# A decoder trunk on one core: order of the first attention scores, the projections' lead and the conditioning jobs

## The chip, the cores and the metric

The kernel runs on one core of a Trainium2 chip. The metric is the device time of one execution in microseconds (us), the median of several runs. A core has TensorE (matmuls, transposes), VectorE, ScalarE, GpSimd, and SyncE, whose queue issues the DMAs here.

## What is computed

One sequence of 512 tokens, width 1024, passes a state-space layer, a shared K/V projection, an attention layer of three dilated branches with 16 heads of 64, and an MLP behind each of the two mixers. Every sub-layer is normalised, shifted and scaled by vectors that come from the conditioning vector `c`, and gated by a third. Cut to what matters here:

```python
def ada_chunks(c, w, b, n):                  # conditioning: c (1, 1024), w (1024, n * 1024)
    m = jax.nn.silu(c) @ w + b
    return jnp.split(m[:, None, :], n, axis=-1)

def dilated_mixer(u, w_q, k_bands, v_bands, w_o):
    q = (u @ w_q).reshape(bsz, seq, N_BRANCHES, N_HEADS, HEAD_DIM)
    for i, (win, dil) in enumerate(DILATED_BRANCHES):
        o, l = dilated_branch(q[:, :, i], k_bands[i], v_bands[i], win // dil, dil)
        ...
    weights = jax.nn.softmax(jnp.stack(lses, axis=-1), axis=-1)
    ...

# layer 1 of reference()
    k_bands, v_bands = shared_kv(h, c, kv_g, kv_ada_w, kv_ada_b, w_kv)
    shift, scale, gate = ada_chunks(c, ada_w[layer, 0], ada_b[layer, 0], 3)
    u = rms_norm(h, ln_g[layer, 0]) * (1.0 + scale) + shift
    h = h + gate * dilated_mixer(u, attn_w_q[j], k_bands, v_bands, attn_w_o[j])
    shift, scale, gate = ada_chunks(c, ada_w[layer, 1], ada_b[layer, 1], 3)
    u = rms_norm(h, ln_g[layer, 1]) * (1.0 + scale) + shift
    h = h + gate * (jnp.square(jax.nn.relu(u @ mlp_w1[layer])) @ mlp_w2[layer])
```

The softmax over the three branches together is computed as one softmax over all their keys.

## The kernel before

Every matrix product of a layer is done as three products of a high and a low part of each operand: `linear_steps` (L813) emits them in steps of three matmuls (L827 to L829) and yields after each. Weights come in blocks of 1 MB through SyncE's queue (L789), are split on ScalarE (L799) and VectorE (L801), and are kept in a pool `W` of 13 buffers, which the projected keys, queries and values share. `next_weights(2)` loads two blocks ahead.

The attention (`attention`, L1174) interleaves two streams on TensorE. One is the **feed**: the projections of V (`proj_v`, for four heads at a time), of keys and queries (`proj_kq`, for a pair of heads: six blocks of eight steps) and at the end of the output (`out_part`). Its generator yields the assumed length of each step, 0.64 or 0.327, and `fill(t)` runs steps until `t` is used up. The other stream is the **heads**: eight pairs, each in four head steps `qb`, one for each block of 128 queries. A head step makes the transposes of the softmax (`attn_turn`, L1142 and L1144, copied by L1147 to L1151), fills, makes the scores of the next head step (`attn_scores`, L1107 and L1115), fills, and multiplies with V (`attn_out`, L1163 and L1170). The scores' softmax runs on VectorE and ScalarE between the scores and the next transposes: mask and maximum (L1122), L1124, the exponential (L1126), the reciprocal (L1129), the normalisation (L1131). `self.mark` is the last normalisation emitted, `self.act_mark` the last exponential.

How much is filled where is set by a few numbers. Before the first scores the feed is run for `KQ + V + AHEAD`, that is through the first V, the first keys and queries and `AHEAD` more. `per` is a twelfth of one pair's share of the feed; `LEFT` is taken from the share of the seventh pair (index 6), and the eighth pair's share has `LEFT - AHEAD`. `PARTS` says how many twelfths stand in each place of a head step.

TensorE's instructions in this stage keep the order in which they are written (`pinned`). For the other engines and for SyncE's queue a scheduler sets the order by simulated time: among the instructions that are ready it takes the one written first. `after(i, j)` makes instruction i stand behind j on its engine. With `self.heads` set, the splits of the weights are put behind the last softmax in this way.

The **late jobs** compute `silu(c) @ w` for 16 blocks of 256 columns (gate2, ada3 and gate3, used after the heads). One job (`ada_jobs`) loads 1 MB into the tiles h4 to h7 in four DMAs (L1471), then works on VectorE: L1482, seven times L1487, a transpose (L1490) into the first loaded tile and a reduction (L1491). After the last job of a vector `finish` (L1527, eight small matmuls, and L1531) ends it. `late_step`, at the end of each head step, emits a pending `finish`, the job loaded at the head step before, and the next load.

Of the kernel before, what the change touches and what calls it, by code (L numbers as in the profile page):

```python
# [12 lines left out]
ALU = mybir.AluOpType  # L13
# [19 lines left out]
PUMPS_END = ((0, 3), (1, 0), (1, 3))  # L33


AHEAD, LEFT, REST = 9.0, 8.4, 2.0

PARTS, PARTS_END = (1.4, 1.6, 0.0), (1.0, 1.0, 1.0)
NEG = -1e30
# [55 lines left out]
class Trunk:  # L95
# [1078 lines left out]
    def attention(self, adaq, adakv, gate):  # L1174
        nc, a = self.nc, self.a
# [173 lines left out]
        def fill(t):  # L1349
            state[0] += t  # L1350
            while state[0] > 0:
                c = next(steps, None)
                if c is None:
                    state[0] = 0.0
                    return
                state[0] -= c

        KQ, V = 6 * 8 * 0.64, 16 * 0.64 + 16 * 0.1 + 64 * 0.327
        with self.pinned(nc.tensor):
            fill(0.327 * 15.5)  # L1360
            self.pumped()
            self.table(AF.Exp, self.act_mark)
            fill(KQ + V + AHEAD - 0.327 * 15.5)
            nxt = self.attn_scores(0, kqs[0][0])
            self.heads = True
            for pair in range(KT):

                per = (KQ + V * (pair % 2) - LEFT * (pair == KT - 2) if pair < KT - 1 else
                       4 * 7 * 0.64 + LEFT - AHEAD - REST) / 12
                po = self.mm_ps()  # L1370
                parts = PARTS if pair < KT - 1 else PARTS_END
                for qb in range(4):
                    pts = self.attn_turn(qb, nxt, kqs[pair][1])
                    fill(per * parts[0])
                    if qb < 3:
                        nxt = self.attn_scores(qb + 1, kqs[pair][0])
                    elif pair < KT - 1:
                        nxt = self.attn_scores(0, kqs[pair + 1][0])
                    fill(per * parts[1])
                    self.attn_out(pair, qb, pts, vs[pair // 2], po)  # L1380
                    if qb == 3:
                        o = ow[pair] = self.t([P, T], f"h{pair}")
                        nc.vector.tensor_copy(o.rearrange("p (b i r) -> p b r i", b=4, r=4),  # L1383
                                              po.rearrange("p (b r i) -> p b r i", b=4, r=4))
                    fill(per * parts[2])
                    self.late_step()
            fill(1000)
# [69 lines left out]
    def ada_jobs(self, w, ncols, n, c, late=False):  # L1457


        nc = self.nc  # L1460
        nk = ncols // P
        part = self.t([P, nk * 4], "apart", 2)
        o, finish = self.ada_columns(part, n, c)

        def load(c0):
            wv = w[:, c0:c0 + 256].rearrange("(k p) n -> p k n", p=P)
            if late:
                raw = []
                for i in range(4):
                    t = self.t([P, 2, 256], f"h{4 + i}")  # L1470
                    nc.sync.dma_start(t, wv[:, 2 * i:2 * i + 2])  # L1471
                    raw += [t[:, j] for j in range(2)]
                return raw
            t = self.w([P, KT, 256])
            i = nc.sync.dma_start(t, wv)
            if self.job_mark is not None:
                self.after(i.ins, self.job_mark, mybir.DependencyClass.Sync)
            return [t[:, k] for k in range(KT)]

        def job(c0, raw):  # L1480
            acc = self.t([P, 256], "aacc")
            i = nc.vector.tensor_scalar(acc, raw[0], self.cs[:, 0:1], None, ALU.mult)  # L1482
            if not self.jobs_started:
                self.jobs_started = True
                self.after(i.ins, self.mark)
            for k in range(1, KT):
                nc.vector.scalar_tensor_tensor(acc, raw[k], self.cs[:, k:k + 1], acc, ALU.mult, ALU.add)  # L1487

            tr = raw[0]
            nc.vector.transpose(tr, acc)  # L1490
            nc.vector.tensor_reduce(part[:, c0 // 32:c0 // 32 + 8], tr.rearrange("p (n i) -> p n i", i=32),  # L1491
                                    mybir.AxisListType.X, ALU.add)
            if c0 + 256 == ncols:
                self.ends.append(finish)

        for c0 in range(0, ncols, 256):
            if late:
                self.late.append((lambda c0=c0: load(c0), lambda raw, c0=c0: job(c0, raw)))
            else:
                self.jobs.append(lambda c0=c0: job(c0, load(c0)))  # L1500
        return o

    def late_step(self):

        ends, self.ends = self.ends, []
        for end in ends:
            end()
        if self.loaded:
            do, raw = self.loaded
            self.loaded = None  # L1510
            do(raw)
        if self.late:
            load, do = self.late.pop(0)
            self.loaded = (do, load())

    def ada_columns(self, part, n, c):

# [252 lines left out]
```

## Time and profile before

| | |
|---|---|
| median of 3 runs | 1573.6 us (1571.99 to 1575.98) |
| the profiled execution | 1572.7 us |
| its span, first to last instruction | 1570.9 us |
| TensorE busy | 1468.5 us, 93% of the span |
| VectorE busy | 945.9 us, 60% |
| ScalarE busy | 569.4 us, 36% |
| GpSimd busy | 134.1 us, 9% |
| DMA | 188.59 MB, mean 120 GB/s |

Times in the views are us from the span's start. A row of a timeline gives start, length, engine, line, operation, output and inputs by the program's names, shapes and count; in square brackets stands how long the engine had been idle before it and what ended that. Matmuls are pipelined: one of 512 columns has a length of 0.39 us, while the next starts 0.23 us after it. The attention stage lies between about 600 and 1180 us.

### The profile page before, as it was taken

How to read it: one execution, taken by the hardware profiler on the slowest of the kernel's cores; microseconds unless marked ns; L12 is line 12 of the kernel's file. 1: busy time of each engine (PE TensorE's matmuls, PEld its weight loads, DVE VectorE, ACT ScalarE, POOL GpSimd, SP SyncE). 2: the span in 40 equal slices, each digit the busy share in tenths (PEclk: the TensorE clock that was granted, in tenths of full speed). 3: DMA queues.
4: the chain of work that ended last, by engine and by line, in shares of the span. 5: the costliest groups of instructions: out<-in, count | busy, mean ns of one | idle time of the engine just before them, and what ended most of it. 6: DMA issues, size and time to landing. Idle time of an engine off the chain costs nothing.

```text
span 1570.9 us, 27064 instructions
## 1 busy us (share of the span) xinstructions
PE 1468.5 (93%) x11540; PEld 1228.3 (78%) x11540; DVE 945.9 (60%) x1641; ACT 569.4 (36%) x989; POOL 134.1 (9%) x112
## 2 busy tenths in 40 slices
PE   2566999999999999979999999999999999999998
PEld 1445789888888888967887888798878888888887
DVE  8989996889874345657774433433558544344322
ACT  5656633424242334421332322332345423232222
POOL 8867100000000001000000000000000000000000
PEclk9888999999999999998999999999999999999999
DMA  9413581976743232354643212221325232332301
GB/s 228 133 55 82 167 236 29 323 230 196 231 143 104 85 121 88 104 164 145 180 141 102 82 55 81 82 82 55 102 84 167 78 111 82 106 99 89 107 1 54
DMA packets 214488, 188.59 MB, mean 120 GB/s; under 512 B 7480, under 2 KB 208352, under 8 KB 214368
## 3 DMA queue, kind: packets, MB, share of 16 engines
q1 hardware_dynamic: 214368, 186.87, 39.2%
q8 instruction: 90, 1.47, 0.4%
q14 instruction: 30, 0.25, 0.0%
HBM read 182.66 MB, written 4.19 MB: 119 GB/s over the span
## 4 chain that ended last, share of the span: by engine, by line
PE 73%; DVE 15%; DMA 7%; issue 3%; ACT 1%; SPq 1%; POOL 0%; DVEq 0%; ACTq 0%
PE mm L827 21%; PE mm L829 20%; PE mm L828 20%; DMA h<-in_ada_w_dram 3%; DVE aacc L1487 2%; DVE W L801 2%; DMA W<-in_attn_w_q_dram 2%; PE mm L1253 1%; PE mm L1254 1%; PE mm L1255 1%; DMA W<-in_mlp_w_dram 1%; PE mm L1170 1%; ACT W L799 1%; PE aux L1142 1%; PE aux L1107 1%
## 5 line engine op out<-in xcount | busy, mean ns | idle before, releaser
L799 ACT CAST W<-W 128x1024 fp32r<-128x1024 f32 (+1 forms) x228 | 223.4, 1030 | 400.2 <-PE mm L828 195.6
L827 PE MATMUL mm<-uz,W 128*128 128x512 f32 (+1 forms) x952 | 360.7, 381 | 3.6 <-DVE h L1383 2.7
L829 PE MATMUL mm<-uz,W 128*128 128x512 f32 (+1 forms) x952 | 358.9, 377 | 3.1 <-DVE W L801 3.1
L801 DVE TENSOR_TENSOR W<-W,W 128x1024 fp32r<-128x1024 f32 (+1 forms) x228 | 265.6, 1196 | 159.1 <-ACT W L799 137.2
L828 PE MATMUL mm<-uz,W 128*128 128x512 f32 (+1 forms) x952 | 358.3, 377 | 2.7 <-DVE uz L749 2.4
L827 PE MATMUL mm<-hid,W 128*128 128x512 f32 (+1 forms) x792 | 300.5, 380 | 0.3 <-ACT hid L1000 0.3
L828 PE MATMUL mm<-hid,W 128*128 128x512 f32 (+1 forms) x792 | 297.4, 376 | 2.5 <-DVE hid L1001 2.5
L829 PE MATMUL mm<-hid,W 128*128 128x512 f32 (+1 forms) x792 | 296.9, 375 | 0.0
L827 PEld LDWEIGHTS mm<-uz,W 128*128 128x128 f32 x952 | 180.2, 190 | 38.0 <-DVE h L1383 2.8
L829 PEld LDWEIGHTS mm<-uz,W 128*128 128x128 f32 x952 | 179.9, 189 | 36.2 <-DVE W L801 3.5
L828 PEld LDWEIGHTS mm<-uz,W 128*128 128x128 f32 x952 | 180.2, 189 | 35.2 <-DVE uz L749 2.8
L828 PEld LDWEIGHTS mm<-hid,W 128*128 128x128 f32 x792 | 150.2, 190 | 29.2 <-DVE hid L1001 3.1
L827 PEld LDWEIGHTS mm<-hid,W 128*128 128x128 f32 x792 | 149.8, 190 | 27.9 <-ACT hid L1000 0.5
L829 PEld LDWEIGHTS mm<-hid,W 128*128 128x128 f32 x792 | 149.9, 189 | 27.2
L852 DVE SCALAR_TENSOR_TENSOR h<-mm,ada,h 128x512 f32<-128x512 f32 (+1 forms) x77 | 54.1, 707 | 146.7 <-PE mm L829 146.6
L1487 DVE SCALAR_TENSOR_TENSOR aacc<-W,cs,aacc 128x256 f32<-128x256 f32 x196 | 95.5, 487 | 4.0
L1126 ACT ACTIVATE sg<-aux,st 128x192 f32<-128x192 f32 (+3 forms) x64 | 36.6, 577 | 154.5 <-DVE st L1124 148.6
L1029 DVE TENSOR_TENSOR sg<-sg 128x512 f32<-128x512 f32 x64 | 43.8, 688 | 55.3 <-ACT uz L1028 55.0
L1027 ACT ACTIVATE sg<-mm 128x512 f32<-128x512 f32 x60 | 35.6, 596 | 112.7 <-PE mm L829 108.5
L1253 PE MATMUL mm<-W,hid 128*128 128x256 f32 x256 | 73.4, 287 | 0.0
L1254 PE MATMUL mm<-W,hid 128*128 128x256 f32 x256 | 72.4, 283 | 0.0
L1255 PE MATMUL mm<-W,hid 128*128 128x256 f32 x256 | 72.4, 283 | 0.0
(329 smaller groups left out, 1699.3 us busy)
## 6 DMA issues: line engine op xcount, KB each, us to landing
W<-in_mlp_w_dram SPq DMA_DIRECT2D x64, 1024.0 KB, 5.4
W<-in_ada_w_dram SPq DMA_DIRECT2D x20, 1024.0 KB, 7.4
h<-in_ada_w_dram SPq DMA_DIRECT2D x64, 256.0 KB, 3.2
W<-in_w_kv_dram SPq DMA_DIRECT2D x12, 1024.0 KB, 5.6
W<-in_w_kv_dram SPq DMA_DIRECT2D x24, 512.0 KB, 4.2
W<-in_attn_w_q_dram SPq DMA_DIRECT2D x24, 512.0 KB, 5.7
W<-in_ssm_w_glu_dram SPq DMA_DIRECT2D x16, 512.0 KB, 5.4
W<-in_kv_ada_w_dram SPq DMA_DIRECT2D x8, 1024.0 KB, 5.6
```

The lines of the kernel that those rows point to most:

```text
L799: h = (nc.gpsimd.tensor_copy if first else nc.scalar.copy)(wh[:, ks], raw[:, ks])
L801: j = eng.tensor_tensor(wl[:, ks], raw[:, ks], wh[:, ks].bitcast(F32), ALU.subtract)
L827: nc.tensor.matmul(o, wh[:, k], uh, start=(start and k == order[0]), stop=False)
L828: nc.tensor.matmul(o, wh[:, k], ul, start=False, stop=False)
L829: self.pe_mark = nc.tensor.matmul(o, wl[:, k], uh, start=False, stop=(stop and k == order[-1])).ins
L852: self.mark = nc.vector.scalar_tensor_tensor(self.h[k][:, cs], src[:, cs], gate[:, k:k + 1], self.h[k][:, cs], ALU.mult, ALU.add).ins
L1029: nc.vector.tensor_tensor(rl, rl, rl, ALU.mult)
L1126: self.act_mark = nc.scalar.activation(p[:, 0:W], ps[:, 0:W], AF.Exp, bias=st[:, 1, e:e + 1], scale=0.125, accum_out=st[:, 2, e:e + 1]).ins
L1253: nc.tensor.matmul(ps[:, j], us[0], wh, start=(k == 0), stop=False)
L1254: nc.tensor.matmul(ps[:, j], us[0], wl, start=False, stop=False)
L1255: nc.tensor.matmul(ps[:, j], us[1], wh, start=False, stop=(k == KT - 1))
L1487: nc.vector.scalar_tensor_tensor(acc, raw[k], self.cs[:, k:k + 1], acc, ALU.mult, ALU.add)
```

## The change

Three things are changed. The first scores are emitted nine steps (9 * 0.64) before the end of the first long fill, and `self.heads` is set before them, not after. `AHEAD` and `LEFT` grow by 3.2 each: the feed runs 3.2 further ahead in the first seven pairs, and is where it was from the eighth on. A late job becomes a generator of two halves. The first half (L1482 and four times L1487) is emitted by a new `late_half`, between the transposes' fill and the next scores; the second half stays in `late_step`. While the heads run, the first instruction of each half is put behind the last normalisation emitted. `late_half` also emits the pending `finish`, which `late_step` did before.

```diff
-AHEAD, LEFT, REST = 9.0, 8.4, 2.0
+AHEAD, LEFT, REST = 12.2, 11.6, 2.0
...
             self.table(AF.Exp, self.act_mark)
-            fill(KQ + V + AHEAD - 0.327 * 15.5)
+            fill(KQ + V + AHEAD - 9 * 0.64 - 0.327 * 15.5)
+            self.heads = True
             nxt = self.attn_scores(0, kqs[0][0])
-            self.heads = True
+            fill(9 * 0.64)
             for pair in range(KT):
...
                     pts = self.attn_turn(qb, nxt, kqs[pair][1])
                     fill(per * parts[0])
+                    self.late_half()
                     if qb < 3:
                         nxt = self.attn_scores(qb + 1, kqs[pair][0])
...
         def job(c0, raw):
+            for _ in job_steps(c0, raw):
+                pass
+
+        def job_steps(c0, raw):
             acc = self.t([P, 256], "aacc")
             i = nc.vector.tensor_scalar(acc, raw[0], self.cs[:, 0:1], None, ALU.mult)
-            if not self.jobs_started:
+            if self.heads or not self.jobs_started:
                 self.jobs_started = True
                 self.after(i.ins, self.mark)
             for k in range(1, KT):
-                nc.vector.scalar_tensor_tensor(acc, raw[k], self.cs[:, k:k + 1], acc, ALU.mult, ALU.add)
+                if k == 5:
+                    yield
+                i = nc.vector.scalar_tensor_tensor(acc, raw[k], self.cs[:, k:k + 1], acc, ALU.mult, ALU.add)
+                if k == 5 and self.heads:
+                    self.after(i.ins, self.mark)
...
             if late:
-                self.late.append((lambda c0=c0: load(c0), lambda raw, c0=c0: job(c0, raw)))
+                self.late.append((lambda c0=c0: load(c0), lambda raw, c0=c0: job_steps(c0, raw)))
...
     def late_step(self):
+
+        if self.loaded:
+            self.some(self.loaded)
+            self.loaded = None
+        if self.late:
+            load, do = self.late.pop(0)
+            self.loaded = do(load())
+
+    def late_half(self):
 
         ends, self.ends = self.ends, []
         for end in ends:
             end()
         if self.loaded:
-            do, raw = self.loaded
-            self.loaded = None
-            do(raw)
-        if self.late:
-            load, do = self.late.pop(0)
-            self.loaded = (do, load())
+            self.some(self.loaded, 1)
```

## Rows read from the trace of the kernel before

**Rows 1.** The page: its span, and each engine's busy time, share and instructions.

```profile
span 1570.9 us, 27064 instructions
PE 1468.5 (93%) x11540; PEld 1228.3 (78%) x11540; DVE 945.9 (60%) x1641; ACT 569.4 (36%) x989; POOL 134.1 (9%) x112
```

**Rows 2.** TensorE's waits, 580 to 1200 us: in total, times, longest.

```profile
PE aux L1142 <- DVE sg L1131: 13.9, 5, 9.3
...
PE aux L1115 <- DVE W L1294: 2.6, 1, 2.6
```

**Rows 3.** TensorE's timeline: the first scores' end and the waits of the heads.

```profile
698.12 0.42 PE L1115 MATMUL aux<-W 64*32 64x32 f32 x32
707.81 0.61 PE L1142 MATMUL aux<-cst,sg 128*32 128x128 f32 x2 [9.27 <-DVE sg L1131]
...
722.09 0.38 PE L1142 MATMUL aux<-cst,sg 128*64 128x128 f32 x2 [1.11 <-DVE sg L1131]
...
735.78 0.63 PE L1142 MATMUL aux<-cst,sg 128*96 128x128 f32 x2 [1.83 <-DVE sg L1131]
...
835.37 0.36 PE L1115 MATMUL aux<-W 64*32 64x32 f32 x16 [2.64 <-DVE W L1294]
...
1137.34 0.41 PE L1142 MATMUL aux<-cst,sg 128*128 128x128 f32 x2 [1.55 <-DVE sg L1131]
```

**Rows 4.** Stretches: length, busy PE, PEld, DVE, ACT, POOL, granted clock, DMA.

```profile
708.00:712.00 4.00, 4.00 (x14) 3.25 (x13) 3.93 (x8) 0.72 (x2) 0.00 (x0) 0.54 0.42 125
735.60:739.10 3.50, 3.32 (x12) 3.00 (x13) 2.50 (x7) 0.83 (x3) 0.00 (x0) 0.52 0.72 193
834.50:841.50 7.00, 6.13 (x30) 4.84 (x31) 6.76 (x19) 0.91 (x4) 0.00 (x0) 0.51 0.02 4
```

**Rows 5.** VectorE's timeline in the first gap.

```profile
700.29 0.33 DVE L1124 TENSOR_SCALAR st<-st 128x1 f32<-128x1 f32 x2
706.13 0.35 DVE L1482 TENSOR_SCALAR aacc<-h,cs 128x256 f32<-128x256 f32 x1 [5.51 <-DMA h<-in_ada_w_dram]
...
707.44 0.54 DVE L1131 TENSOR_SCALAR sg<-sg,st 128x192 f32<-128x192 f32 x2
```

**Rows 6.** VectorE's timeline: a job's first step ahead of later waits of TensorE.

```profile
719.18 0.35 DVE L1482 TENSOR_SCALAR aacc<-h,cs 128x256 f32<-128x256 f32 x1 [2.31 <-DMA h<-in_ada_w_dram]
...
832.71 0.35 DVE L1482 TENSOR_SCALAR aacc<-h,cs 128x256 f32<-128x256 f32 x1 [5.99 <-DMA h<-in_ada_w_dram]
833.10 1.53 DVE L1487 SCALAR_TENSOR_TENSOR aacc<-h,cs,aacc 128x256 f32<-128x256 f32 x3
834.54 0.68 DVE L1294 COPY W<-mm 128x512 f32<-128x512 f32 x1
```

**Rows 7.** L1482: VectorE's idle time before it; L1471: its DMAs' landing.

```profile
  DMA h<-in_ada_w_dram: 34.1, 13
...
DMA to landing us min/median/max: 2.7/3.2/6.4
```

**Rows 8.** Two matmuls in sequence; VectorE in an undisturbed softmax (eighth pair).

```profile
696.92 0.39 PE L827 MATMUL mm<-uz,W 128*128 128x512 f32 x1
697.15 0.39 PE L828 MATMUL mm<-uz,W 128*128 128x512 f32 x1
...
1167.54 0.70 DVE L1122 CUSTOM_DVE_ANT_0 aux<-aux,bz 128x512 f32<-128x512 f32 x1 [1.80 <-PE aux L1115]
...
1170.91 0.88 DVE L1131 TENSOR_SCALAR sg<-sg,st 128x512 f32<-128x512 f32 x2
```

**Rows 9.** VectorE's timeline before the late wait in the seventh pair.

```profile
1130.71 2.36 DVE L801 TENSOR_TENSOR W<-W,W 128x1024 fp32r<-128x1024 f32 x2 [0.78 <-PE aux L1115]
```

**Rows 10.** SyncE's queue; one weight block's split on VectorE; its first matmul.

```profile
712.95 24.77 SPq L1471 DMA_DIRECT2D h<-in_ada_w_dram  x10
...
947.32 2.36 DVE L801 TENSOR_TENSOR W<-W,W 128x1024 fp32r<-128x1024 f32 x2 [8.53 <-PE aux L1115]
...
963.39 0.39 PE L827 MATMUL mm<-hid,W 128*128 128x512 f32 x1
```

## The prediction

> **What bounds the kernel now.** I read the page first: TensorE is busy for 93% of the span [rows 1]. With so full an engine only its idle time and its slow time can be won, so the second view is the list of TensorE's waits in the attention stage. Two lines of it belong to the head loop: the transposes at L1142 wait for the normalisation L1131 for 13.9 us in 5 waits, and the scores at L1115 wait 2.6 us for a copy of a projection, L1294 [rows 2]. The third view, TensorE's timeline, places them. The first scores end at 698.54 (the row's start and length) and the first transpose starts at 707.81 after 9.27 us of nothing. The next two transposes wait 1.11 and 1.83 us, the scores of the third pair 2.64 us, and one late transpose, in the seventh pair, 1.55 us [rows 3]. The fourth view is the granted clock. After three of these gaps it stands near half, the lower level of 1.2 GHz: 0.54 from 708, 0.52 from 735.6, 0.51 from 834.5 [rows 4]. Busy time times the missing share is what that cost: 4.00 x 0.46 = 1.84 us, 3.32 x 0.48 = 1.59 us, 6.13 x 0.49 = 3.00 us.
>
> The last view, VectorE's timeline, says why. In the first gap the pair of L1124 ends at 700.62 and VectorE then has nothing but the first step of a conditioning job (L1482) at its head, which waits 5.51 us for its load. The normalisation L1131 stands behind it and ends near 708 [rows 5]. The same holder, with 2.31 us, stands ahead of the second transpose. At 832.71 it holds VectorE for 5.99 us, three more steps of the job follow, and only then comes the copy L1294 for which the scores wait [rows 6]. Over the whole kernel these first steps of the late jobs hold VectorE for 34.1 us in 13 waits [rows 7]. So the cause of the gaps is not VectorE's load but its order: a job whose operands are not there is queued ahead of the softmax.
>
> **The change part by part, against the profiled execution (1572.7 us; 1.8 us of it outside the span; it is 0.9 us under the median of 1573.6, so the result can be read against either).** No arithmetic is added or removed: same matmuls, same 16 late jobs, same loads.
>
> *First scores earlier, nine steps behind them.* The scores are emitted 9.0 - (12.2 - 9 x 0.64) = 2.56 of the code's us sooner in the stream of projections, four steps, and nine steps now stand between them and their transposes. A step is three matmuls at 0.23 us start to start [rows 8], so the cover is 27 x 0.23 = 6.1 us. The chain it must cover, undisturbed, is 4.3 us for the widest scores (from their end near 1167.45, when VectorE is released, to 1171.79) [rows 8]; the first scores are the narrowest. The job's first step is pinned behind the last normalisation emitted, so it can't be ahead of this one, and the first job even waits for the second scores. The gap goes: 9.27 us and the slow 1.84 us behind it, 11.1 us. What moves with the nine steps: one call for weights, whose loads and splits keep their place behind the first softmax (the pins use the same marks), one ScalarE copy and one VectorE copy of the projection (L1294 shows 0.68 us [rows 6]). The 6.1 - 4.3 = 1.8 us of spare cover hides that; without it the copy would cost 0.7 us.
>
> *Jobs in halves, pinned.* A job step takes 1.53 / 3 = 0.51 us [rows 6]. A half is five of these, or three with the transpose and reduction, about 2.4 us each. Job s's first half follows the same normalisation as job s-1's second half, and the load stands between them, because the second half frees the tiles. Gone are the 1.11 and 1.83 us and the slow 1.59 us: 4.5 us. New is this: after each normalisation VectorE has 2.4 us of second half, a load landing in 3.2 us in the median and 6.4 at most [rows 7], and 2.4 us of first half. With the chain of 4.3 us that makes 12.3 us, against a step of 735.78 - 722.09 - 1.83 = 11.9 us in a pair without V [rows 3]. So the first half hangs 0.4 us over the next scores in the median. The transposes' cover takes that; a late load exceeds it. Pairs with V have longer fills. Nine turns are exposed (the rest of pair 0 and the start of pair 1, most of pair 2 and the start of pair 3, two in pair 4). Each can lose between nothing and 1.11 us, which is what a hold of 2.31 us cost in the row nearest to this [rows 3, 6]: 0 to 10 us. I take a third, 3 us, since only loads landing later than the median exceed the cover.
>
> The Trainium skill, page "DMA: Bandwidth & Descriptors", section "Latency and other measured facts", gives a fixed cost of about 2 us for a DMA. By that figure a half would be done 1.2 us earlier and this term would be nothing, the time 1553; the row has 3.2 us, and I keep it.
>
> The jobs now run until the fifth pair, where before the last began at 832.71 [rows 6]. Their results are first needed behind the last head. The three closing matmul groups (L1527) move from a step's end to before the scores. TensorE would wait there only if a second half were late, and the transposes and a fill lie between. I cost that at nothing, with the bound of one reduction's delay, about 2 us, in pair 4.
>
> *Projections further ahead.* All steps up to the seventh pair run 12.2 - 9.0 = 3.2 of the code's us ahead, five steps, 15 x 0.23 = 3.4 us. The scores of the third pair, which waited 2.64 us for a copy made late by the same holder [rows 3, 6], win both ways: 2.64 + 3.00 slow = 5.6 us. The price stands in the seventh pair. LEFT takes the same 3.2 out of its twelve shares, so of the fill that covers a softmax 1.6 x 3.2 / 12 = 0.43 is missing, in whole steps 0.7 us. There the cover is short already: one transpose waits 1.55 us [rows 3], because 2.36 us of a weight split ran ahead of its reduction [rows 9]. Three turns lose between 0 and 2 us each, and a fall of the clock can follow. Against that, a split may also land in another place and the 1.55 us go: bounds -1.5 to +8, I take 1.5 us, two turns losing a whole step each.
>
> The sum: 11.1 + 4.5 + 5.6 - 3.0 - 1.5 = 16.7 us, 1572.7 - 16.7 = 1556.0.
>
> **The rivals.** *VectorE stays held.* The pin orders a half behind one normalisation but not behind its load, so it can still stand ahead of the next reduction. All nine turns then pay 1.11 us: 7 us more than in the sum, 1563, with a slow stretch 1565. For it speaks that the order before was made with loads taken as sooner than they land (13 holds [rows 7]); against it, that these halves are half as long. The Trainium skill, page "PSUM — Partial Sum Buffer", section "Engine vs sequencer instructions", calls VectorE's queue a strict FIFO. The row of 5.51 us agrees: a ready normalisation behind it did not pass.
>
> *The first gap only shrinks.* If something else takes the job's place and the chain stays at 9.3 us, the 6.1 us of cover leave 3.2 us and the slow 1.84: saved 6.1 instead of 11.1, 1561.
>
> *The seventh pair turns bad.* Three turns at 2 us and a slow stretch of 1.6 us: 7.6 in place of 1.5, 1562.
>
> *The weights come late; slower than before.* SyncE's queue takes loads in order, and ten of the jobs' loads already held it for 24.77 us [rows 10]. Now a job's load waits for a half that is pinned to a step, and this goes on into the pairs where the reserve is thinnest: there a split ends at 949.68 and is used at 963.39, 13.7 us later [rows 10]. A hold as long as 24.77 us in front of such a weight makes TensorE wait 11 us, with a slow stretch 13. Two such loads take back 26 us, more than the 21 us won: 1577. It decides from the second such load on. Against it: the hold of 24.77 us fell on larger reserves and no wait for weights was seen [rows 2].
>
> *First and third together* (all turns pay, the seventh pair bad): 1570, no change to be told.
>
> **How the numbers follow.** Forecast 0.60 (its own range 1550 to 1561), held VectorE 0.13, smaller first gap 0.07, bad seventh pair 0.08, two together 0.06, late weights 0.06. Predicted is 1556. Range: below, all costs at nothing and the late gap gone (1572.7 - 21.2 - 1.5 = 1550), a little under for runs that differ; above, the held VectorE with its slow stretch, 1566. That leaves out 0.12 and some of the tails. A measurement of this kernel can tell about 0.3%, 4.7 us: faster 0.88, same 0.06 (the two together), slower 0.06.
>
> **What would show it.** TensorE's wait at the first transpose gone and the granted clock full from 640 to 1170; no wait of the third pair's scores for L1294; the jobs' first steps one per head step, each behind a normalisation, the last near the fifth pair. Right in size if the waits for L1131 sum to 5 us or less. Wrong if a weight's split ends the idle time, or if waits for L1131 stand in every step of the even pairs.

## The result and the profile after

The changed kernel takes 1554.82 us (median of 4 runs, 1553.16 to 1557.32), against 1573.22 us of the kernel before in the same comparison: a ratio of 0.9882, with a 95% interval of 0.9861 to 0.9903. It is faster by 18.4 us; the prediction was 1556 us, with a range of 1550 to 1566. Its profiled execution took 1553.4 us, 19.3 us less than that of before. Measured twice more, on other chips, the same kernel took 1557.64 and 1555.67 us (e8_changed, e12_changed_again), 15.2 and 17.6 us less than the kernel before beside it, so differences of 1 or 2 us between kernels that were not measured side by side mean little.

The page of the changed kernel, span and engines as in [rows 1]:

```profile
span 1551.6 us, 27063 instructions
PE 1460.4 (94%) x11540; PEld 1224.5 (79%) x11540; DVE 943.8 (61%) x1641; ACT 569.1 (37%) x989; POOL 134.1 (9%) x112
```

The work is the same to the instruction on TensorE and VectorE. TensorE's busy time is 8.1 us shorter with the same matmuls; the three slow stretches of [rows 4], which are gone, are 6.4 us of that. The other 11 us were idle time. The waits of TensorE from 580 to 1200 us, changed kernel (total, times, longest), against [rows 2]:

```profile
PE aux L1142 <- DVE sg L1131: 4.5, 4, 1.6
...
PE mm L827 <- DVE h L1385: 2.7, 1, 2.7
PE aux L963 <- DVE rcol L959: 1.3, 1, 1.3
```

13.9 us of waits for the normalisation have become 4.5 us, and the line of the scores that waited for a copy (L1115 for L1294) is gone. TensorE's timeline of the changed kernel, where [rows 3] had the gaps:

```profile
693.75 0.42 PE L1115 MATMUL aux<-W 64*32 64x32 f32 x32
700.36 0.38 PE L1142 MATMUL aux<-cst,sg 128*32 128x128 f32 x2
...
736.39 0.41 PE L1142 MATMUL aux<-cst,sg 128*128 128x128 f32 x2 [0.89 <-DVE sg L1131]
...
819.16 0.43 PE L1115 MATMUL aux<-W 64*32 64x32 f32 x32
...
854.65 0.39 PE L1142 MATMUL aux<-cst,sg 128*96 128x128 f32 x2 [0.94 <-DVE sg L1131]
...
867.74 0.41 PE L1142 MATMUL aux<-cst,sg 128*128 128x128 f32 x2 [1.09 <-DVE sg L1131]
...
1118.25 0.41 PE L1142 MATMUL aux<-cst,sg 128*128 128x128 f32 x2 [1.57 <-DVE sg L1131]
```

The first transposes and the third pair's scores carry no bracket, so TensorE did not stand idle before them. Three smaller waits are new, and the late one of the seventh pair is the old one. The stretches of the attention in the changed kernel (length; busy PE, PEld, DVE, ACT, POOL; clock; DMA), against [rows 4]:

```profile
640.00:690.00 50.00, 50.00 (x275) 43.66 (x274) 26.45 (x40) 19.00 (x30) 0.00 (x0) 1.00 0.36 103
690.00:740.00 50.00, 49.11 (x560) 38.87 (x560) 28.41 (x72) 15.58 (x33) 0.00 (x0) 1.00 0.33 100
740.00:850.00 110.00, 110.00 (x1233) 92.45 (x1232) 65.40 (x151) 33.44 (x64) 0.00 (x0) 1.00 0.45 134
850.00:960.00 110.00, 107.97 (x1194) 90.79 (x1194) 68.46 (x164) 32.75 (x64) 0.00 (x0) 1.00 0.46 132
960.00:1090.00 130.00, 130.00 (x1573) 109.01 (x1574) 54.55 (x124) 42.98 (x81) 0.00 (x0) 1.00 0.28 81
1090.00:1156.00 66.00, 63.44 (x1096) 50.00 (x1094) 38.27 (x97) 27.83 (x63) 0.00 (x0) 1.00 0.30 94
```

The granted clock is full throughout, and busy PE fills each stretch but for those waits and, in the last, under 1 us of smaller ones. To see where the 19.3 us fell I take the stage between two fixed places, the first matmul of L1253 and the last of L1170. Before they lie at 630.8 and 1176.6, after at 629.2 and 1155.7 (the first and last start of these two lines). The stage is 19.3 us shorter. What lies ahead of it was 1.6 us shorter in this execution, and what lies behind 1.6 us longer; these two cancel.

Why the first gap is gone stands in VectorE's timeline of the changed kernel, against [rows 5]:

```profile
694.26 0.37 DVE L1122 CUSTOM_DVE_ANT_0 aux<-aux,bz 128x192 f32<-128x192 f32 x1 [6.48 <-PE aux L1115]
...
696.06 0.17 DVE L1129 RECIPROCAL st<-st 128x2 f32<-128x2 f32 x1 [0.87 <-ACT sg L1126]
696.26 0.55 DVE L1131 TENSOR_SCALAR sg<-sg,st 128x192 f32<-128x192 f32 x2
```

VectorE waits for the scores (6.48 us, ended by L1115) and not for a load, and the chain ends at 696.81, 2.6 us behind the scores; the nine steps, 6.2 us from the scores' end to the transposes, cover it with 3.6 us to spare.

### The profile page after: what moved, and what is told of

It reads as the page before. It is cut to its first block, busy times and chain, and to the rows that moved or that the text cites. A ratio compares the mean times of both kernels' runs of the same rounds, so it can differ in the third digit from the quotient of the medians.

```text
span 1551.6 us, 27063 instructions
## 1 busy us (share of the span) xinstructions
PE 1460.4 (94%) x11540; PEld 1224.5 (79%) x11540; DVE 943.8 (61%) x1641; ACT 569.1 (37%) x989; POOL 134.1 (9%) x112
## 4 chain that ended last, share of the span: by engine, by line
PE 82%; DVE 12%; DMA 2%; issue 2%; ACT 1%; SPq 0%; POOL 0%; DVEq 0%; ACTq 0%
PE mm L827 22%; PE mm L828 22%; PE mm L829 22%; PE mm L1253 2%; PE mm L1254 2%; PE mm L1255 2%; DVE W L801 1%; PE mm L1170 1%; DMA h<-in_ada_w_dram 1%; PE aux L1107 1%; PE aux L1142 1%; PE mm L1163 1%; DVE W L563 1%; PE aux L1115 1%; DVE aacc L1495 1%
## 5 line engine op out<-in xcount | busy, mean ns | idle before, releaser
L801 DVE TENSOR_TENSOR W<-W,W 128x1024 fp32r<-128x1024 f32 (+1 forms) x228 | 266.3, 1196 | 148.3 <-ACT W L799 123.1
L1253 PE MATMUL mm<-W,hid 128*128 128x256 f32 x256 | 73.5, 287 | 0.0
```

The costliest lines, as they stand in the source:

```text
L801: j = eng.tensor_tensor(wl[:, ks], raw[:, ks], wh[:, ks].bitcast(F32), ALU.subtract)
L1253: nc.tensor.matmul(ps[:, j], us[0], wh, start=(k == 0), stop=False)
```

## Experiments

The theory: what costs time is not the jobs' work but their place in VectorE's in-order queue. An instruction whose operands are still on the way stands ahead of a softmax or of a copy, and that costs TensorE whatever its cover does not hide. The rivals: the added cover does it all; the lead does it; the halves do it.

### One part at a time

```diff
# e1_pins_only: the changed kernel without its other two parts
-AHEAD, LEFT, REST = 12.2, 11.6, 2.0
+AHEAD, LEFT, REST = 9.0, 8.4, 2.0
-            fill(KQ + V + AHEAD - 9 * 0.64 - 0.327 * 15.5)
-            self.heads = True
+            fill(KQ + V + AHEAD - 0.327 * 15.5)
             nxt = self.attn_scores(0, kqs[0][0])
-            fill(9 * 0.64)
+            self.heads = True
# e2_scores_first: the kernel before with these lines of the change alone
# e3_ahead_only: the kernel before with AHEAD, LEFT = 12.2, 11.6 alone
# e4_no_ahead: the changed kernel with AHEAD, LEFT = 9.0, 8.4
```

> The kernel before, with the jobs in halves and pinned alone; first scores where they were, AHEAD 9.0. Theory (the job's place in VectorE's queue makes the gaps): the first transpose waits only the bare chain, about 2.7 us instead of 9.27, and no slow stretch follows; the second and third transposes lose their 1.11 and 1.83 us, some 1 us may come back elsewhere; the third pair's scores keep part of their 2.64 us, since the lead is short. Saved 6.6 + 1.8 + 4.5 - 2.9 = 10 us, up to 15 if the third pair's wait goes too: 1558 to 1563. Rival (the nine steps of cover are what cures the first gap): it stays near 9 us, saved 4 us or less, 1569 or more.

> The kernel before, with the first scores nine steps ahead alone; jobs whole and free, AHEAD 9.0. Theory: a job still stands in VectorE's queue next to the first softmax, now ahead of its reduction, so the chain is still longer than 4 us; 6.1 us of it are covered, 0 to 3 us remain; the waits of 1.11, 1.83, 2.64 us and their slow stretches stay as a group of about 10 us, perhaps at other turns. Saved 6 to 11 us: 1562 to 1567. Rival (pins are not needed, the cover does it all): 18 us saved, 1555.

> The kernel before, with AHEAD and LEFT 3.2 larger alone. Theory: the third pair's scores lose their wait of 2.64 us and the slow 3.0 us behind it, the first gap stays near 9 us, the seventh pair costs 0 to 1.5 us: saved 2 to 6 us, 1567 to 1571. Rival (that wait, too, is the job's place and moves with it): it comes back at another turn, 1572 to 1575.

> The changed kernel with AHEAD and LEFT back at 9.0 and 8.4. Theory with the lead as a part of its own: the third pair's scores wait again, up to 2.64 us and a slow stretch of 3.0 us: 1557 to 1560. Rival (the pins alone had taken away the holder of that copy): no wait there, the same as the changed kernel, 1554 to 1556.

The kernel before took 1572.04 us in this comparison.

| kernel | us | ratio to before (95%) |
|---|---|---|
| pins and halves alone | 1563.65 | 0.9948 (0.9929 to 0.9967) |
| scores first alone | 1566.98 | 0.9967 (0.9955 to 0.9980) |
| lead alone | 1568.44 | 0.9975 (0.9964 to 0.9985) |
| pins and scores first, no lead | 1560.29 | 0.9930 (0.9913 to 0.9947) |

The second and third came in the range of the theory, the first and fourth 0.7 and 0.3 us above it; the four rivals, in which one part does all or nothing, fell. The three parts alone bring 8.4, 5.1 and 3.6 us, together about what the whole change does. With the pins alone the first transposes wait only for the bare chain (TensorE's timeline, e1_pins_only). The clock is at 0.50 for 3.4 us behind it, where I had expected no slow stretch:

```profile
700.43 0.40 PE L1142 MATMUL aux<-cst,sg 128*32 128x128 f32 x2 [2.47 <-DVE sg L1131]
```

A wait came back elsewhere too, and it was more than the 1 us expected: 3.42 us in the fifth pair (976.99), behind a weight's split, with a clock of 0.53 after it. Before the change the same transposes waited 0.16 us.

With the scores first alone 2.54 us of the gap are left, again with a slow stretch (0.52 for 3.4 us). The scores end at 692.69. Ahead of their reduction stand a weight's split, which waits for ScalarE's cast, and the first five steps of a job, whose load is there (VectorE's timeline, e2_scores_first):

```profile
693.75 1.22 DVE L801 TENSOR_TENSOR W<-W,W 128x1024 fp32r<-128x1024 f32 x1 [5.18 <-ACT W L799]
694.89 0.35 DVE L1483 TENSOR_SCALAR aacc<-h,cs 128x256 f32<-128x256 f32 x1
...
696.29 2.04 DVE L1488 SCALAR_TENSOR_TENSOR aacc<-h,cs,aacc 128x256 f32<-128x256 f32 x4
698.25 0.36 DVE L1122 CUSTOM_DVE_ANT_0 aux<-aux,bz 128x192 f32<-128x192 f32 x1
```

The third pair's scores wait even longer than before. VectorE's timeline there repeats [rows 6], with the same holder and the same copy behind it, and TensorE's wait of 4.01 us at 830.12 follows:

```profile
827.45 0.35 DVE L1483 TENSOR_SCALAR aacc<-h,cs 128x256 f32<-128x256 f32 x1 [5.70 <-DMA h<-in_ada_w_dram]
827.84 1.53 DVE L1488 SCALAR_TENSOR_TENSOR aacc<-h,cs,aacc 128x256 f32<-128x256 f32 x3
829.28 0.69 DVE L1294 COPY W<-mm 128x512 f32<-128x512 f32 x1
```

With the lead alone that wait is gone, but the first gap is 10.09 us, and its holder is another: VectorE's timeline (e3_ahead_only) has a weight's split ahead of the first reduction, waiting for ScalarE's cast, which waits for its own load.

```profile
705.17 2.36 DVE L801 TENSOR_TENSOR W<-W,W 128x1024 fp32r<-128x1024 f32 x2 [4.90 <-ACT W L799]
707.45 0.35 DVE L1482 TENSOR_SCALAR aacc<-h,cs 128x256 f32<-128x256 f32 x1
...
708.23 0.36 DVE L1122 CUSTOM_DVE_ANT_0 aux<-aux,bz 128x192 f32<-128x192 f32 x1
```

So a job is one holder among others: a weight's split that waits for its transfer does the same. In the changed kernel these weights are called for behind the first scores, with `heads` set, so their split is pinned; here they are called for ahead of the scores. The jobs have a hand in this gap as well: on SyncE's queue the weights' loads of 697.10 and 700.16, the last before that cast, stand behind three loads each of the late jobs.

Without the lead (e4_no_ahead) the third pair's scores wait 1.77 us, as expected, with no fall of the clock; VectorE is held for 6.01 us by a job's first step ahead of their copy, pins or no pins. The kernel gains 11.8 us over the kernel before, where the changed kernel gained 15.2 to 18.4 in its three measurements. Most of the difference is two waits that I had not expected: 2.07 us in the third pair (854.43, with a clock of 0.51 behind it) and 3.66 us in the fifth, with 3.4 us at a clock of 0.50 behind it (TensorE's timeline, then VectorE's ahead of it):

```profile
976.53 0.38 PE L1142 MATMUL aux<-cst,sg 128*64 128x128 f32 x2 [3.66 <-DVE sg L1131]
```

```profile
970.97 2.36 DVE L801 TENSOR_TENSOR W<-W,W 128x1024 fp32r<-128x1024 f32 x2 [2.32 <-ACT W L799]
973.25 0.56 DVE L1122 CUSTOM_DVE_ANT_0 aux<-aux,bz 128x384 f32<-128x384 f32 x1
```

Here, too, a split stands ahead of the reduction, after 2.32 us in which VectorE waited for its cast. It is the wait that the pins alone had (3.42 us).

### What is left of the waits: halves, pins, loads

```diff
# e5_whole_job: the changed kernel, the job in one piece in late_step, one pin
         def job_steps(c0, raw):
+            yield
...
-                if k == 5:
-                    yield
                 i = nc.vector.scalar_tensor_tensor(acc, raw[k], self.cs[:, k:k + 1], acc, ALU.mult, ALU.add)
-                if k == 5 and self.heads:
-                    self.after(i.ins, self.mark)
# e6_no_pins: the changed kernel, both pins off
-            if self.heads or not self.jobs_started:
+            if not self.jobs_started:
...
-                if k == 5 and self.heads:
-                    self.after(i.ins, self.mark)
# e7_no_loads: the changed kernel, load() of a late job returns the first job's tiles
+            if late and self.late_raw is not None:
+                return self.late_raw
```

> The changed kernel itself once more, to stand beside the others on the same chip. Both theories: 1553 to 1556, and VectorE's holds at the jobs' first steps about 42 us in sum, while TensorE waits for L1131 for some 4.5 us.

> The changed kernel with each job in one piece in late_step, its first step pinned behind the last normalisation; still one job in a head step. Theory (what is left of the waits is a hold, because the load stands between two halves that follow the same normalisation): now a load has most of a head step to land, the holds fall from 42 us to under 10, the waits for L1131 in the first three pairs fall from 2.9 us to 0 to 1: 1551 to 1554. Rival (halves are needed, since 4.9 us in one piece push the next reduction): waits of 1 to 2 us in most even-pair turns, 1558 to 1565.

> The changed kernel without the two pins of a job; halves, scores first and lead stay. Theory (the pins keep the job from the softmax): in VectorE's queue a whole job stands ahead of the first reduction again, with its hold; part of it is covered by the nine steps, waits for L1131 of 3 to 8 us in the first pairs, 1558 to 1565. Rival (cover and lead are enough): 1553 to 1556.

> The changed kernel with the loads of all late jobs but the first left out (the later jobs compute on what the first left in the tiles, so gate2, ada3 and gate3 are not the reference's). Theory (the waits of 0.89, 0.94 and 1.09 us come from the holds of 2.26, 2.94 and 1.70 us at a first step): holds and these waits go, 3 us saved, 1551 to 1553. Rival (they come from VectorE's work, the halves and the weights' splits): they stay, 1553 to 1556.

The kernel before took 1572.83 us in this comparison.

| kernel | us | ratio to before (95%) | VectorE held by late jobs | TensorE waits for L1131 |
|---|---|---|---|---|
| changed, again | 1557.64 | 0.9905 (0.9888 to 0.9921) | 42.2 us, 14 | 5.0 us, 4 |
| whole job, one pin | 1554.85 | 0.9888 (0.9873 to 0.9903) | 0 | 1.6 us, 1 |
| no pins | 1570.31 | 0.9983 (0.9973 to 0.9992) | 33.1 us, 11 | 13.6 us, 6 |
| no loads after the first | 1552.08 | 0.9870 (0.9855 to 0.9885) | 0 | 1.6 us, 1 |

The changed kernel came 1.6 us above what I had expected and the whole job 0.9 us above it; the whole job is 2.8 us under the changed kernel, and no loads 5.6 us, both by the medians.

The pins carry the change. Without them 2.5 us are left of the gain, less than the theory had (1558 to 1565, with waits of 3 to 8 us where 13.6 came). A whole job stands ahead of the first reduction, but its load is there and the nine steps just cover it: the first transposes, at 701.99, do not wait. The old gap is back one step later. VectorE's timeline there (e6_no_pins), a job's first step waiting for its load between a reduction and the normalisation that TensorE needs, and then TensorE's row:

```profile
713.97 0.56 DVE L1122 CUSTOM_DVE_ANT_0 aux<-aux,bz 128x384 f32<-128x384 f32 x1
...
717.48 0.35 DVE L1488 TENSOR_SCALAR aacc<-h,cs 128x256 f32<-128x256 f32 x1 [2.19 <-DMA h<-in_ada_w_dram]
...
719.31 0.74 DVE L1131 TENSOR_SCALAR sg<-sg,st 128x384 f32<-128x384 f32 x2
```

```profile
719.87 0.60 PE L1142 MATMUL aux<-cst,sg 128*64 128x128 f32 x2 [6.55 <-DVE sg L1131]
```

With the loads taken away the three new waits go, as the theory has it: they are holds, not work. They were 3.43 us in the profile of e8_changed, and the stage from L1253 to L1170 is 3.4 us shorter (523.5 against 526.9). This run also takes the jobs' loads off SyncE's queue, so by itself it leaves open whether the holds or the queue did it. In the changed kernel the three holds ahead of them are these (VectorE's timeline of the changed kernel):

```profile
727.71 0.36 DVE L1488 TENSOR_SCALAR aacc<-h,cs 128x256 f32<-128x256 f32 x1 [2.26 <-DMA h<-in_ada_w_dram]
...
849.47 0.35 DVE L1488 TENSOR_SCALAR aacc<-h,cs 128x256 f32<-128x256 f32 x1 [2.94 <-DMA h<-in_ada_w_dram]
...
860.20 0.35 DVE L1488 TENSOR_SCALAR aacc<-h,cs 128x256 f32<-128x256 f32 x1 [1.70 <-DMA h<-in_ada_w_dram]
```

With the job in one piece they go as well, although VectorE does all of the work and the queue has every load: the load then has a whole head step to land. So the holds explain them, and the queue's load alone does not. The halves, then, were not needed for what the pins do; they put the load between two halves that follow the same normalisation. One wait came in their place, TensorE's timeline of e5_whole_job:

```profile
976.64 0.25 PE L1538 MATMUL aux<-apart,cst 128*32 128x8 f32 x8 [1.93 <-DVE apart L1498]
```

### Whole jobs, with the closing matmuls back in their place

```diff
# e9_ends_back and, again, e11_ends_back_again: e5_whole_job, with the closing matmuls at the step's end
     def late_step(self):
 
+        ends, self.ends = self.ends, []
+        for end in ends:
+            end()
         if self.loaded:
...
     def late_half(self):
 
-        ends, self.ends = self.ends, []
-        for end in ends:
-            end()
# e10_whole_no_ahead: e9_ends_back with AHEAD, LEFT = 9.0, 8.4
# e12_changed_again: the changed kernel
```

> The whole-job kernel with the closing matmuls back at the end of the head step, as before the change. Theory (its one new wait, 1.9 us of the closing matmuls for the last job's reduction in the fifth pair, comes from their earlier place): that wait goes and no other comes: 1551 to 1554, faster than before and than the changed kernel. Rival (another order of the queue brings a wait elsewhere): 1555 or more.

> The same with AHEAD and LEFT at 9.0 and 8.4: what the lead is worth once no job holds VectorE. Theory (the lead itself pays where the third, fifth and seventh pair's first scores need a copy made just before): the third pair's scores wait 0.5 to 1.8 us, with or without a slow stretch: 1 to 4 us more than with the lead, 1553 to 1557. Rival (most of the lead's gain was the shift of the jobs against the weights' splits, whose 3.7 us wait came back without the lead): no difference or faster, 1551 to 1553.

> The kernel with whole jobs and the closing matmuls back in their place, once more, beside the changed kernel on the same chip. Theory (holds and closing wait cost the changed kernel 2.9 to 3.4 us and slow stretches nothing): 3 us under the changed kernel, 1551 to 1553. Rival (the gain was the chip's): within 1 us of it.

> The changed kernel beside it: 1554 to 1557; its waits for L1131 4.5 to 5 us in sum, of which 1.6 in the seventh pair.

With the closing matmuls back in their place the kernel takes 1551.59 us (0.9874, 0.9859 to 0.9888), and in the second comparison 1553.44 us (0.9867, 0.9850 to 0.9884) beside 1555.67 us (0.9888, 0.9870 to 0.9907) of the changed kernel. It beats the kernel before clearly. That it beats the changed kernel by 2.2 us in that second comparison, where 3 were expected, is the reading of the medians; the intervals of the two overlap. The profiles agree with it: the stage from L1253 to L1170 is 523.5 and 523.6 us long in its two, and 526.5, 526.9 and 527.4 us in the three of the changed kernel. In the last of these the waits for L1131 were 5.4 us, a little over the 4.5 to 5 expected. Where the changed kernel lost 2.0 us, in its row from 850 to 960, e9_ends_back has this one:

```profile
850.00:960.00 110.00, 110.00 (x1272) 92.61 (x1271) 68.10 (x158) 31.31 (x60) 0.00 (x0) 1.00 0.45 130
```

Without the lead it is at 1555.46 us (0.9890, 0.9873 to 0.9906), 3.9 us more by the medians, while the intervals overlap; the stage of its profile is 529.5 us, 6.0 more. The theory that the lead pays at the first scores of a pair fell here: no scores wait in this kernel. What it waits for is the normalisation, 1.54 us in the third pair and 2.17 us in the fifth, and both times a split stands ahead of the reduction (VectorE's timeline, e10_whole_no_ahead, third pair):

```profile
835.86 2.36 DVE L801 TENSOR_TENSOR W<-W,W 128x1024 fp32r<-128x1024 f32 x2 [5.77 <-ACT W L799]
838.13 0.56 DVE L1122 CUSTOM_DVE_ANT_0 aux<-aux,bz 128x384 f32<-128x384 f32 x1
```

## The prediction, step by step

**The first gap, 11.1 us: right, and by its own reasons.** The gap and the slow stretch are gone. The chain was 2.6 us, shorter than the 4.3 us taken as its bound. The pins alone leave 2.47 us, the cover alone 2.54 us, each with a slow stretch. Cover and lead without pins (e6_no_pins) leave nothing there, but 6.55 us one step later: it is the pins that keep the gap from moving on.

**Jobs in halves: 4.5 us won, 3 us given back; right in sum, and the mechanism as named.** 0.89 + 0.94 + 1.09 = 2.92 us came back, each behind a hold of 1.7 to 2.9 us. But it was three turns at about 1 us, not nine at a third of that, so that the sum came out as taken is luck in part. The forecast that a hold would remain was more right than I had put it: VectorE's holds at these first steps rose, from 34.1 us in 13 waits [rows 7] to 42.3 us in 14. What changed is where they stand. The four waits ahead of which they stood before sum to 14.9 us, of which 2.5 are the bare chain of the first softmax that the pins alone leave, so the holds cost TensorE about 12 us; pinned behind a normalisation they cost it 3. The load's landing stayed at 3.1 us in the median. By the 2 us of the Trainium skill (page "DMA: Bandwidth & Descriptors", section "Latency and other measured facts") the prediction would have put this term at nothing, and the measurement has it at 2.9. The two figures are not the same thing, though: what the Trainium skill gives there is a fixed cost, and the landing measured here has the moving of 256 KB in it.

**The closing matmuls, nothing, with a bound of 2 us: right for the change, and the bound was real.** With whole jobs the wait appeared, at the place named (fifth pair), with 1.93 us.

**Projections further ahead, 5.6 us at the third pair: the time went, but the reason was half wrong.** I gave it to the lead and the pins both, and either does most of it alone. The lead alone takes that wait away (e3_ahead_only), the pins alone bring it down to 0.53 us with no slow stretch after it, and with whole jobs and no lead there is none; of the kernels with pins only e4_no_ahead has more, 1.77 us. In the profiles the lead is worth more than that one wait: 8.6 us of the stage with halves (535.1 us in e4_no_ahead, 526.5 in the changed kernel) and 6.0 with whole jobs. In the third and fifth pair it keeps a weight's split from standing ahead of a reduction. That these waits would come with the pins and without the lead could not be read from the rows of before, and no run shows which of its effects (the splits' place in the queue, or the loads' time) does it.

**The seventh pair, 1.5 us lost: mis-sized, and in part lucky.** It lost nothing. Its wait is 1.57 us where it was 1.55, behind the same split (L801 from 1111.62, the reduction at 1113.90), with the same cover. I had counted a whole step's loss in two other turns, and both did lose that cover. The third turn, 0.7 us shorter, had 1.0 us to spare and kept 0.3. The second, 0.9 us shorter, had no more than 0.1 to spare. It was saved because the split that had run ahead of its reduction before now ran ahead of its scores (from 1089.75, the scores at 1094.02). VectorE's timeline of the kernel before, where the scores of that turn end at 1111.57:

```profile
1109.98 2.36 DVE L801 TENSOR_TENSOR W<-W,W 128x1024 fp32r<-128x1024 f32 x2 [1.85 <-ACT W L799]
...
1112.65 0.56 DVE L1122 CUSTOM_DVE_ANT_0 aux<-aux,bz 128x384 f32<-128x384 f32 x1
```

The prediction had named such a move as a chance, but for the late wait alone.

**The sum.** 21.2 us of gaps and slow stretches gone, 2.9 back, nothing at the seventh pair, 1.1 us of small waits gone that I had not counted (0.25 and 0.16 at products with V and transposes, 0.7 for ScalarE's L1309) and one of 0.35 us new (for ScalarE's L1277, at 1113.34): 19.1, against 19.3 measured in the stage. The profiled execution, 1553.4, lies 2.6 us under the 1556.0 of the sum: 1.5 of the seventh pair, 0.8 of the small waits and 0.3 that I can't place.

**The rivals.** None of them came in the changed kernel, and what was to show the forecast did: no wait at the first transposes, a full clock, no wait of the third pair's scores, and waits for L1131 of 4.5 us (5.0 and 5.4 in the two other profiles, where 5 was the limit). A smaller first gap is what the scores first alone give; VectorE held is what it is without pins, though at 1570 us and not at 1563 to 1565. Late weights came in no run: in the attention no list has a wait of TensorE for a split's result.

**Not foreseen:** a wait of 1.29 us behind the attention, where a split (2.35 us) now runs ahead of the last sum of squares, and 3.5 us at a clock of 0.52 after it. It is in each of the three profiles of the changed kernel.

## To carry to other kernels

When an engine on the path waits for one that is half idle, look at what stands at the head of that one's queue; if it waits for a transfer, its place is the fault and not its length. Pin background work behind the latency-bound chain, and give its load the whole time between two pins: one piece per step with the load between the steps, not two halves with the load between them. After a change of order, look for the next holder: here it was a weight's split in five of the variants (e1 to e4 and e10), at the first reduction or in the third and fifth pair.

## Of the hardware, not expected

The same gap does not always cost the same. Behind the attention TensorE waits 2.73 us for the same copy (L1385 in the changed kernel) in each profile. In one profile of the changed kernel the clock stayed full after it, in another execution of the same kernel it was at 0.50 for 3.4 us (the stretch behind the wait, first the profile of the result, then e8_changed):

```profile
1158.70:1162.10 3.40, 3.40 (x15) 2.83 (x16) 0.69 (x1) 1.31 (x2) 0.00 (x0) 1.00 0.90 283
```

```profile
1160.70:1164.10 3.40, 3.06 (x7) 2.48 (x8) 0.98 (x2) 0.88 (x2) 0.00 (x0) 0.50 0.91 292
```

The wait of 1.29 us was followed by the low level, 1.2 GHz, in both (0.52 and 0.55), while the 1.57 us of the seventh pair never was, in any profile. Within one execution, e10_whole_no_ahead, the wait of 1.54 us had a clock of 0.67 in the 3.4 us after it and the longer one of 2.17 us a clock of 1.00. So the length of a gap alone does not tell whether the clock falls; in a sum, the slow stretch behind a gap of 1 to 3 us is a term with both ends, here 0 to 1.7 us.
